# Turning 30 column groups of two up projections to tokens-as-rows, with VectorE squares and DMAs in front of the convolution

## The chip, the cores and the metric

One core of one Trainium2 chip runs the whole program in one launch. The metric is the device time of that launch in microseconds: the median of three runs of the kernel before is 1923.41 us (1923.33 to 1925.26). One further execution was taken by the hardware profiler. All durations in this document come from that profiled execution, and times in it are counted from the start of its span.

## What is computed

A trunk of two layers over 256 tokens and 2048 channels, all in float32. Each layer has a mixer (layer 0 pools over time, layer 1 attends), a residual and a layer norm, and then the part that the change is about: a gated feed-forward network with a causal convolution of width 3 over time between the up projection and the gate, again with a residual and a layer norm.

```python
def conv_ffn(h, w_up, conv_w, conv_b, w_down):
    S = h.shape[1]
    u = h @ w_up                                  # 256 x 2048 times 2048 x 11008
    up = jnp.pad(u, ((0, 0), (CONV_WIDTH - 1, 0), (0, 0)))
    c = conv_b + up[:, 0:S] * conv_w[0]
    for j in range(1, CONV_WIDTH):
        c = c + up[:, j:j + S] * conv_w[j]        # token t sees tokens t, t-1, t-2 of its own channel
    gate, val = jnp.split(c, 2, axis=-1)
    return (jax.nn.silu(gate) * val) @ w_down     # 256 x 5504 times 5504 x 2048
```

Products are as exact as float32: each weight and each activation is split into a high part and a low part, and three products (high by high, high by low, low by high) are added up in PSUM.

## The kernel before, in words

**Units and groups.** The work is a list of units. A unit is one piece of a weight matrix, mostly 512 rows by 512 columns (1 MB). Four units with the same 512 columns make a group, whose sums stay in PSUM until the last unit is done; then a function called `post` takes them out. Per unit, SyncE's queue loads the piece into one of three `raw` buffers (L69), ScalarE makes the high part `wh` (L86), VectorE the low part `wl` (L87), and TensorE multiplies. There are four `wh` and four `wl` buffers, so the split of unit i+3 is issued ahead of unit i, and it can start once TensorE has done unit i-1.

**Two forms of a group.** In the form with channels as rows (`group`, `mm_quad`, mode "ab"), the weight is what TensorE holds still: for each 128 x 128 block, L181 streams the high and the low half of the activations (512 columns), and L183 streams the high half past the low part of the weight (256 columns). The result has channels on partitions and tokens along the row, in four PSUM banks. In the form with tokens as rows (`group_tm`, `tm_block`), the activations are held still and the weight streams, three times 512 columns for each 128 channels and each half of the tokens (L206 to L208). The result has 128 tokens on partitions and 512 channels along the row, in two banks, t0 and t1. The up projections use the first form, the down projections (but for one) the second.

**The feed-forward part.** `ffn` runs up(0), up(1), up(2), then the down projection of their products, then up(3) to up(5) and their down projection, then 6 and 7, then 8 to 10. Each up(q) is two groups, the gate's and the value's. Here "gate q" and "value q" name them. `evac` brings the sums to an SBUF tile `u` (ScalarE copies the one half, L574, VectorE adds the other, L575), `conv` does the convolution (four L583 on ScalarE, eight L587 on VectorE), then SiLU on the gate (L599), gate times value (L620), and the split of the product into `g` (L266 on ScalarE, L262 on VectorE), which the down projection holds still.

**What sets the order.** Each engine does its instructions in the order in which the program lists them, and waits where it must. `later(n, f)` lists f behind the matmuls of the n-th unit from now; `before[i]` lists it ahead of those of unit i, behind the splits that `ahead(i)` lists. Value groups 2, 5, 7 and 10 come right ahead of a down projection, so their convolution is listed without delay (`later(0, ...)`, L626); the others follow one unit later. `turns` lets the first units of two down groups alternate: for up to three q's, the last q is first needed in the fourth unit, and for two q's (6 and 7) in the third.

**Layer norm.** `resid_last` ends in `chain` (L392 on): four small matmuls put mean and mean square into one PSUM bank, ScalarE squares and takes a root (L400, L402), and VectorE makes `rm` (L401, L403, L404). The next group's matmuls use that bank again, so they wait for L404, its last reader. The first groups behind a norm run in a mode "x" on values that are not yet normalised, and `norm_evac` (L439) puts mean and deviation in at the end.

**Existing turns.** `to_tokens` (L658) and `to_features` (L672) turn the residual between the two layouts: four VectorE transposes, each of 32 x 32 squares, into a tile, then 16 DMAs of 32 partitions each, issued by GpSimd, that put the squares in place.

Of the kernel before, what the change touches and what calls it, by code (L numbers as in the profile page):

```python
# [33 lines left out]
def trunk(ctx: ExitStack, tc: tile.TileContext, x, pool_w_in, pool_w_grp, pool_scale, pool_w_out,  # L34
# [102 lines left out]

    def phi(ps):
        return untwine(ps[:, :T])
# [124 lines left out]
    def split_act(dst, src):  # L264
        n = src.shape[1]
        A.copy(dst[:, 0:n, 0, :T], src)  # L266
        lo_part(dst, src, n)
# [7 lines left out]
    invd = const.tile([P, P], F32, name="invd")  # L275
    ones4 = const.tile([P, P], F32R, name="ones4")
# [72 lines left out]
    def shift(s, first, lay, which):  # L349
        ps = bank("shift")  # L350
        PE.matmul(ps[:, :T], ones4, s, start=True, stop=True)
        cs = lnp.tile([P, T], F32R, name="cs", tag="cs")
        A.copy(cs, ps[:, :T])
# [37 lines left out]
    def chain(ps, lay, which, after):  # L391
# [10 lines left out]
        A.activation(t2[:, 1, :], t2[:, 1, :], AF.Sqrt, bias=epst)  # L402
        V.reciprocal(rm[:, 0, :], t2[:, 1, :])  # L403
        V.tensor_tensor(rm[:, 1, :], mean, rm[:, 0, :], OP.mult)  # L404
        mb, rb = mr.to_broadcast([P, 4, T]), rs.to_broadcast([P, 4, T])
        g0 = 32 * which

        def spread():
            for i in range(4):
                PE.matmul(ps[:, i * P:i * P + P], one1, dg[:, i, :], start=True, stop=True)  # L410
            A.copy(rm.rearrange("p a t -> p (a t)"), ps)
            norm(0)
# [26 lines left out]
    def norm_evac(ps, nb, tmp, dst):  # L439
# [3 lines left out]
        for m0 in range(0, nb, 2):  # L443
            ts = [(m, tmp()) for m in range(m0, min(nb, m0 + 2))]
            for m, t in ts:
                V.tensor_tensor(apart2(t), phi(ps[m]), apart2(ST["rs"]), OP.mult)
            for m, t in ts:
                V.scalar_tensor_tensor(t, ST["mr"], wgb[:, m, 0:1], t, op0=OP.mult, op1=OP.subtract)
                A.activation(dst(m), t, AF.Identity, scale=-1.0, bias=wgb[:, m, 1:2])
# [15 lines left out]
    def pool_post(g):  # L465
        def post(ps):
# [3 lines left out]
            for m in range(4):  # L470
                pm = apart2(p[:, m, PADW:])
                A.copy(pm, phi(ps[m]))
                if g < 3:
                    V.tensor_tensor(pm, pm, plo(ps[m]), OP.add)
# [13 lines left out]
            def two():  # L488
                pooled_q[g] = quad_tile("pooled")
                split_act(pooled_q[g], po)  # L490
# [17 lines left out]
    def x_quad(q, halves=(0, 1)):  # L508
# [4 lines left out]
        for half in halves:  # L513
# [5 lines left out]
            pv2 = ps.rearrange("p (k t) -> p k t", k=2)  # L519
            s = slice(2 * half, 2 * half + 2)  # L520
            if q == 0 and half == 1:
                V.tensor_copy(XC[q][:, s, 0, :T], pv2)
            else:
                A.copy(XC[q][:, s, 0, :T], pv2)
            V.tensor_tensor(XC[q][:, s, 1, :T], pv2, XC[q][:, s, 0, :T].bitcast(F32), OP.subtract)
            before.setdefault(min(q + 1, 3), []).append(lambda s=s, pv2=pv2: A.copy(H[q][:, s, :], pv2))
# [26 lines left out]
    def ffn(lay):  # L553
# [3 lines left out]
        def pads():  # L557
            u = pools["ffn"].tile([P, 4, 2 + T], F32, name="u", tag="t4")
            V.memset(u[:, :, 0:2], 0.0)
            return u  # L560

        def evac(ps, nb, mode):
            fp = pools["ffn"]
            u = pads()

            def tmp():
                return fp.tile([P, T], F32, name="ut", tag="t1", bufs=4)

            if mode == "x":
                norm_evac(ps, nb, tmp, lambda m: u[:, m, 2:])  # L570
                return u
            for m in range(nb):
                t = apart2(tmp())
                A.copy(t, plo(ps[m]))  # L574
                V.tensor_tensor(apart2(u[:, m, 2:]), phi(ps[m]), t, OP.add)  # L575
            return u

        def conv(u, blk0, nb):
            cv = cvec[lay]
            c = pools["ffn"].tile([P, 4, T], F32, name="c", tag="t4")  # L580
            for m in range(nb):
                j = blk0 + m
                A.activation(c[:, m, :], u[:, m, 2:], AF.Identity, scale=cv[:, 2, j:j + 1], bias=cv[:, 3, j:j + 1])  # L583
            for i in (1, 0):
                for m in range(nb):
                    j = blk0 + m
                    V.scalar_tensor_tensor(c[:, m, :], u[:, m, i:i + T], cv[:, i, j:j + 1], c[:, m, :],  # L587
# [3 lines left out]
        def gate_post(q, nb, mode):  # L591
            def post(ps):
                u = evac(ps, nb, mode)

                def two():
                    c = conv(u, 4 * q, nb)

                    def three():
                        A.activation(c[:, :nb], c[:, :nb], AF.Silu)  # L599
                        gates[q] = c  # L600

                    later(1, three)

                later(1, two)
            return post

        def val_post(q, nb, mode):
            def post(ps):
                later(1 if q == 0 else 0, lambda: val_chain(q, nb, mode, ps))
            return post  # L610

        def val_chain(q, nb, mode, ps):
            u = evac(ps, nb, mode)

            def two():
                c = conv(u, NF + 4 * q, nb)

                def three():
                    s = gates.pop(q)
                    V.tensor_tensor(s[:, :nb], s[:, :nb], c[:, :nb], OP.mult)  # L620
                    gq[q] = quad_tile("g")
                    split_act(gq[q], s[:, :nb])
# [3 lines left out]
            later(0 if q in (2, 5, 7, 10) else 1, two)  # L626
# [65 lines left out]
    def store(c, t):  # L692
        nc.sync.dma_start(out[0, t * P:(t + 1) * P, 512 * c:512 * c + 512], HT[c][:, t, :])

    def tm_post(c, first, last, back=False):
        def post(t, ps, half=None):
# [6 lines left out]
            if back and t == 1:  # L703
                later(2 + 3 * c, lambda: to_features(c))
# [341 lines left out]
```

## Time and profile before

| | |
|---|---|
| median of 3 runs | 1923.41 us |
| the profiled execution's own time | 1923.13 us |
| its span, first to last instruction | 1921.3 us |
| granted TensorE clock | 1.000 |
| VectorE (DVE) busy | 1409.5 us, 73% |
| ScalarE (ACT) busy | 1012.8 us, 53% |
| GpSimd (POOL) busy | 176.1 us, 9% |
| DMA queue of SyncE | 381.71 MB, 59.3% of the 16 engines' time |

A row of the groups' table reads: line, engine, operation, output <- inputs, shape, count | busy us, mean ns of one | idle us of the engine ahead of them, and what ended the idle time. A row of a timeline reads: start us, us, engine, line, operation, count, and in brackets the idle time ahead and what ended it. In both, PE is TensorE, PEld its weight load, SPq the queue of SyncE. Matmuls overlap in their drawn durations, so their pace is read from start to start.

### The profile page before, as it was taken

To read this page: it belongs to the slowest core of one execution; us is meant where nothing else is said; L and a number is where in the kernel's file an instruction comes from. 1 tells how busy PE (TensorE), PEld (TensorE's weight loads), DVE (VectorE), ACT (ScalarE), POOL (GpSimd) and SP (SyncE) were. 2 spreads that over 40 slices of the span, in tenths; PEclk is the share of its full clock that TensorE was granted. 3 is DMA by queue.
4 is the path that set the end of the run, shared out by engine and by line. 5 is a ranking of instruction groups with operands and counts; after the bars stand their busy time and mean duration, and the time that the engine had idled before them with its cause. 6 is when DMAs were issued, how large, how long until landed. Compare 5 with 4: busy or idle time off the path is not lost.

```text
span 1921.3 us, 28253 instructions
## 1 busy us (share of the span) xinstructions
PE 1914.9 (100%) x11542; PEld 1748.8 (91%) x11542; DVE 1409.5 (73%) x1760; ACT 1012.8 (53%) x1115; POOL 176.1 (9%) x326
## 2 busy tenths in 40 slices
PE   9999999999999999999999999999999999999999
PEld 9999999899989989999989889999889988989997
DVE  7869888757755767789876767888756765775677
ACT  6545675445535535555644445576535543544553
POOL 2000003300000033000033210001410000000000
PEclk9999999999999999999999999999999999999999
DMA  8665557765565576656566655556865566555564
GB/s 279 227 205 197 176 192 246 231 208 198 197 217 200 188 231 212 197 181 219 174 216 214 201 167 193 189 189 206 252 221 197 198 204 212 198 197 200 184 213 148
DMA packets 204513, 392.61 MB, mean 204 GB/s; under 512 B 11630, under 2 KB 22020, under 8 KB 204128
## 3 DMA queue, kind: packets, MB, share of 16 engines
q1 hardware_dynamic: 194240, 381.71, 59.3%
q0 software_dynamic: 10144, 9.11, 2.3%
q8 instruction: 90, 1.47, 0.3%
q14 instruction: 39, 0.32, 0.0%
HBM read 380.01 MB, written 2.10 MB: 199 GB/s over the span
## 4 chain that ended last, share of the span: by engine, by line
PE 97%; DVE 2%; DMA 0%; issue 0%; SPq 0%; ACT 0%; DVEq 0%
PE acc L181 42%; PE acc L183 21%; PE t L206 8%; PE t L207 8%; PE t L208 8%; PE acc L187 2%; PE acc L185 2%; PE acc L186 2%; DVE wl L87 1%; PE acc L172 0%; PE o L894 0%; PE s L835 0%; DVE xp L386 0%; DMA raw<-in_pool_w_in_dram 0%; DVE fold L325 0%
## 5 line engine op out<-in xcount | busy, mean ns | idle before, releaser
L87 DVE TENSOR_TENSOR wl<-raw,wh 128x2048 fp32r<-128x2048 f32 (+2 forms) x374 | 815.6, 2187 | 398.2 <-ACT wh L86 397.4
L181 PE MATMUL acc<-xc,wh 128*128 128x512 f32 x3072 | 1009.1, 383 | 0.0
L86 ACT CAST wh<-raw 128x2048 fp32r<-128x2048 f32 (+2 forms) x374 | 679.7, 1825 | 484.3 <-PE acc L181 214.0
L183 PE MATMUL acc<-xc,wl 128*128 128x256 f32 x3072 | 835.6, 272 | 0.0
L181 PEld LDWEIGHTS acc<-xc,wh 128*128 128x128 f32 x3072 | 577.6, 188 | 83.6 <-DVE o L897 0.5
L183 PEld LDWEIGHTS acc<-xc,wl 128*128 128x128 f32 x3072 | 589.8, 192 | 0.4
L206 PE MATMUL t<-wh,g 128*128 128x512 f32 x590 | 222.8, 378 | 0.0
L207 PE MATMUL t<-wl,g 128*128 128x512 f32 x590 | 222.8, 378 | 0.0
L208 PE MATMUL t<-wh,g 128*128 128x512 f32 x590 | 222.8, 378 | 0.0
L587 DVE SCALAR_TENSOR_TENSOR c<-u,cv,c 128x256 f32<-128x256 f32 x344 | 141.9, 479 | 0.6
L208 PEld LDWEIGHTS t<-wh,g 128*128 128x128 f32 x590 | 111.5, 189 | 15.6
L206 PEld LDWEIGHTS t<-wh,g 128*128 128x128 f32 x590 | 111.5, 189 | 15.6
L207 PEld LDWEIGHTS t<-wl,g 128*128 128x128 f32 x590 | 111.6, 189 | 15.5
L669 POOL DMA_DIRECT2D ht<-hb x128 | 73.7, 583 | 563.5 <-DVE hb L663 497.5
L185 PE MATMUL acc<-xp,wh 128*128 128x258 f32 x384 | 105.7, 275 | 0.8 <-DVE rm L404 0.8
L186 PE MATMUL acc<-xp,wh 128*128 128x258 f32 x384 | 105.7, 275 | 0.0
L187 PE MATMUL acc<-xp,wl 128*128 128x258 f32 x384 | 105.2, 274 | 0.0
L574 ACT COPY ut<-acc 128x256 f32<-128x256 f32 x156 | 56.2, 372 | 81.5 <-PE acc L183 81.5
L583 ACT ACTIVATE c<-u,cv 128x256 f32<-128x256 f32 x172 | 89.4, 594 | 0.4 <-DVE u L575 0.4
L181 PE MATMUL acc<-o,wh 128*128 128x512 f32 x256 | 84.5, 383 | 0.0
L181 PE MATMUL acc<-mixed,wh 128*128 128x512 f32 x256 | 84.0, 382 | 0.0
L185 PEld LDWEIGHTS acc<-xp,wh 128*128 128x128 f32 x384 | 72.9, 190 | 1.0 <-DVE rm L404 1.0
(220 smaller groups left out, 1985.8 us busy)
## 6 DMA issues: line engine op xcount, KB each, us to landing
raw<-in_ffn_w_up_dram SPq DMA_DIRECT2D x160, 1024.0 KB, 4.9
raw<-in_ffn_w_down_dram SPq DMA_DIRECT2D x80, 1024.0 KB, 5.2
raw<-in_pool_w_out_dram SPq DMA_DIRECT2D x16, 1024.0 KB, 5.1
raw<-in_shared_w_k_dram SPq DMA_DIRECT2D x16, 1024.0 KB, 5.1
raw<-in_attn_w_q_dram SPq DMA_DIRECT2D x16, 1024.0 KB, 5.4
raw<-in_shared_w_v_dram SPq DMA_DIRECT2D x16, 1024.0 KB, 5.7
raw<-in_attn_w_o_dram SPq DMA_DIRECT2D x16, 1024.0 KB, 5.2
raw<-in_pool_w_in_dram SPq DMA_DIRECT2D x12, 1024.0 KB, 6.6
```

The costliest lines, as they stand in the source:

```text
L86: A.copy(h, r)
L87: V.tensor_tensor(l, r, h.bitcast(F32), OP.subtract)
L181: PE.matmul(ps[m], h[:, k, c], q[:, k, :, :T].rearrange("p l (a c) -> p l c a", a=2), start=st, stop=False)
L183: PE.matmul(ps[m][:, :T], l[:, k, c], cols(k, 0), start=False, stop=sp)
L185: PE.matmul(ps[m][:, :n], h[:, k, c], cols(k, 0), start=st, stop=False)
L186: PE.matmul(ps[m][:, :n], h[:, k, c], cols(k, 1), start=False, stop=False)
L187: PE.matmul(ps[m][:, :n], l[:, k, c], cols(k, 0), start=False, stop=sp)
L206: PE.matmul(ps, xh, hk, start=first and k == 0, stop=False)
L207: PE.matmul(ps, xh, lk, start=False, stop=False)
L208: PE.matmul(ps, xl, hk, start=False, stop=last and k == nk - 1)
L583: A.activation(c[:, m, :], u[:, m, 2:], AF.Identity, scale=cv[:, 2, j:j + 1], bias=cv[:, 3, j:j + 1])
L587: V.scalar_tensor_tensor(c[:, m, :], u[:, m, i:i + T], cv[:, i, j:j + 1], c[:, m, :], op0=OP.mult, op1=OP.add)
```

## The change

In both layers, 15 of the 22 groups of the up projection take the form with tokens as rows: the gates of q = 1 to 9 and the values of q = 1, 3, 4, 6, 8 and 9. Groups of q = 0 (mode "x") and of q = 10 (narrower), and the values 2, 5 and 7, stay as they were.

A group with tokens as rows has to be turned for the convolution. `turn_up` transposes 32 x 32 squares out of the two PSUM banks into a tile `b` (four VectorE transposes), then issues 16 DMAs on GpSimd's queue, 32 KB each, into `u`. The convolution of such a group is listed four units later, so behind the whole of the next group.

So that the DMAs move long runs, tokens are held in another order everywhere: within each 128, token 4k+j stands at place 32j+k. A tile `u` has six runs of 64 columns: a token's predecessor stands one run ahead, and two extra runs at the start are filled by one new ScalarE copy per group. Loading, pooling, masks and the final store follow that order; pooling goes through plain token order and back. The split of products is done in two halves of the tokens.

Besides, the root of the norm at the end of layer 0 (`which == 1`) is listed ahead of the next unit's matmuls instead of at once; `ut` takes two buffers instead of four; ones4 goes; `to_features` is listed at units 2, 5, 7, 10 instead of 2, 5, 8, 11; and pool sizes change.

```diff
@@ chain @@
-        A.activation(t2[:, 1, :], t2[:, 1, :], AF.Sqrt, bias=epst)
-        V.reciprocal(rm[:, 0, :], t2[:, 1, :])
-        V.tensor_tensor(rm[:, 1, :], mean, rm[:, 0, :], OP.mult)
+        def root():
+            A.activation(t2[:, 1, :], t2[:, 1, :], AF.Sqrt, bias=epst)
+            V.reciprocal(rm[:, 0, :], t2[:, 1, :])
+            V.tensor_tensor(rm[:, 1, :], mean, rm[:, 0, :], OP.mult)
+
+        if which == 0:
+            root()
+        else:
+            before.setdefault(state["done"] + 1, []).append(root)
@@ split of a product @@
-    def split_act(dst, src):
+    def split_half(dst, t, src):
         n = src.shape[1]
-        A.copy(dst[:, 0:n, 0, :T], src)
-        lo_part(dst, src, n)
+        h, l = (dst[:, 0:n, i, t * P:t * P + P].rearrange("p m (j k) -> p m j k", j=4) for i in range(2))
+        A.copy(h, src)
+        V.tensor_tensor(l, src, h.bitcast(F32), OP.subtract)
@@ ffn @@
+        def turn_up(u):
+            b = pools["ffn"].tile([P, 4, 4, 2, 32], F32, name="b", tag="b", bufs=1)
+
+            def part(t, ps):
+                src = ps.rearrange("p (h i b a) -> p a h i b", a=2, h=2, i=4)
+                dst = b[:, :, :, t, :].rearrange("p i (a h) b -> p a h i b", a=2)
+                for a in range(2):
+                    V.transpose(dst[:, a], src[:, a])
+
+            def move():
+                v = b.rearrange("p i m t b -> p i (m t b)")
+                w = u.rearrange("p j m q -> p j (m q)")
+                for i in range(4):
+                    for j in range(4):
+                        nc.gpsimd.dma_start(w[32 * i:32 * i + 32, 2 + j, :], v[32 * j:32 * j + 32, i, :])
+            return part, move
 
         def conv(u, blk0, nb):
             cv = cvec[lay]
-            c = pools["ffn"].tile([P, 4, T], F32, name="c", tag="t4")
+            A.copy(u[:, 0:2, 0:nb, 1:], u[:, 4:6, 0:nb, :63])
+            c = pools["ffn"].tile([P, 4, 4, 64], F32, name="c", tag="c")
...
+        def post_tokens(q, chain):
+            st = []
+
+            def post(t, ps):
+                if t == 0:
+                    u = runs()
+                    st.extend([u, *turn_up(u)])
+                st[1](t, ps)
+                if t == 1:
+                    st[2]()
+                    chain(q, 4, st[0], 4)
+            return post
 
         def up(q):
             nb = min(4, NF - 4 * q)
-            x0 = q == 0
-            mode = "x" if x0 else "ab"
-            group(w_up, rows4, 512 * q, nb * P, psrcs if x0 else xsrcs, gate_post(q, nb, mode),
-                  mode=mode)
-            group(w_up, rows4, FF + 512 * q, nb * P, psrcs if x0 else xsrcs, val_post(q, nb, mode),
-                  mode=mode)
+            mode = "x" if q == 0 else "ab"
+            for c0, chain in ((512 * q, gate_chain), (FF + 512 * q, val_chain)):
+                if q > 0 and nb == 4 and (chain == gate_chain or q not in (2, 5, 7)):
+                    group_tm(w_up, rows4, c0, 512, xsrcs, post_tokens(q, chain))
+                    continue
+                n = 1 if chain == gate_chain or q not in (2, 5, 7, 10) else 0
+                post = post_features(q, nb, mode, chain, n)
```

**How instructions move, place 1: VectorE around the end of value 7 in layer 0**, right ahead of the down projection of 6 and 7. Before, from the split of the last unit that is listed ahead, to the low half of `g`:

```order
L87 TENSOR_TENSOR wl_6115<-raw_6035,wh_6114 128x2048
L559 MEMSET u 128x4x2
L575 TENSOR_TENSOR u<-acc,ut 128x256 x4
L587 SCALAR_TENSOR_TENSOR c<-u,cv_592,c 128x256 x8
L87 TENSOR_TENSOR wl_6180<-raw_6074,wh_6179 128x2048
L620 TENSOR_TENSOR c<-c 128x1024
L262 TENSOR_TENSOR g<-c,g 128x4x256
```

The same stretch in the changed kernel (L621 is the convolution, L591 the evacuation, L643 gate times value, L274 the low half):

```order
L87 TENSOR_TENSOR wl_5860<-raw_5781,wh_5859 128x2048
L621 SCALAR_TENSOR_TENSOR c<-u,cv_590,c 128x4x64 x8
L568 MEMSET u 128x8
L591 TENSOR_TENSOR u<-acc,ut 128x2x4x32 x4
L621 SCALAR_TENSOR_TENSOR c<-u,cv_590,c 128x4x64 x8
L87 TENSOR_TENSOR wl_5940<-raw_5819,wh_5939 128x2048
L643 TENSOR_TENSOR c<-c 128x1024
L274 TENSOR_TENSOR g<-c,g 128x4x128 x2
```

The first eight convolution steps there are those of gate 7, which came 15 us earlier before; they now stand between the split and the evacuation of value 7. Values 2 and 5 have the same order. On ScalarE the same place holds, in the changed kernel:

```order
L86 CAST wh_5859<-raw_5781 128x2048
L613 COPY u<-u 128x8x63
L617 ACTIVATE c<-u,cv_590 128x4x64 x4
L590 COPY ut<-acc 128x256 x4
L613 COPY u<-u 128x8x63
L617 ACTIVATE c<-u,cv_590 128x4x64 x4
L86 CAST wh_5939<-raw_5819 128x2048
L630 ACTIVATE c<-c 128x1024
L273 CAST g<-c 128x4x128 x2
```

The new copy L613 stands ahead of each set of four L617, and the gate's SiLU (L630) has moved behind the next split.

**Place 2: the norm at the end of layer 0.** Before, ScalarE has, around the square and the root of the variance:

```order
L86 CAST wh_8246<-raw_8107 128x2048
L86 CAST wh_8300<-raw_8180 128x2048
L400 ACTIVATE var<-acc 128x256
L402 ACTIVATE var<-var,epst 128x256
L86 CAST wh_8365<-raw_8244 128x2048
L86 CAST wh_8422<-raw_8298 128x2048
```

In the changed kernel:

```order
L86 CAST wh_7921<-raw_7782 128x2048
L86 CAST wh_7975<-raw_7855 128x2048
L405 ACTIVATE var<-acc 128x256
L86 CAST wh_8037<-raw_7919 128x2048
L409 ACTIVATE var<-var,epst 128x256
L86 CAST wh_8097<-raw_7973 128x2048
```

One split has moved between the square and the root. VectorE has the same there, with the low half of that split between the variance and the reciprocal:

```order
L87 TENSOR_TENSOR wl_7976<-raw_7855,wh_7975 128x2048
L406 TENSOR_TENSOR var<-acc,var 128x256
L87 TENSOR_TENSOR wl_8038<-raw_7919,wh_8037 128x2048
L410 RECIPROCAL rm<-var 128x256
L411 TENSOR_TENSOR rm<-acc,rm 128x256
```

Before, L401, L403 and L404 followed each other directly, and that split came behind them.

**Place 3: GpSimd's queue, from the first feed-forward part to the second.** The changed kernel has, besides loads of constants:

```order
L608 DMA u<-b 32x256 x32
L713 DMA ht<-hb 32x8x32 x16
L608 DMA u<-b 32x256 x16
L713 DMA ht<-hb 32x8x32 x32
L1040 IOTA mk 32x128 x4
L713 DMA ht<-hb 32x8x32 x16
L1040 IOTA mk 32x128 x8
L608 DMA u<-b 32x256 x128
L726 DMA h<-fb 32x8x32 x32
```

Before, the rows of `u` (L608) were not there and the 64 moves of `ht` followed each other with three IOTAs among them. The moves of gate 2 (the second L608 row) now stand behind the first 16 moves of `ht`.

More of the change, by code (lines that the diff above doesn't have):

```diff
@@ L350, in shift @@
         ps = bank("shift")
-        PE.matmul(ps[:, :T], ones4, s, start=True, stop=True)
+        PE.matmul(ps[:, :T], invr, s, start=True, stop=True)
         cs = lnp.tile([P, T], F32R, name="cs", tag="cs")
-        A.copy(cs, ps[:, :T])
+        A.activation(cs, ps[:, :T], AF.Copy, scale=4.0)
         cb = cs.bitcast(F32).unsqueeze(1).to_broadcast([P, 4, T])
@@ L489, in two @@
                 pooled_q[g] = quad_tile("pooled")
-                split_act(pooled_q[g], po)
+                for t in range(2):
+                    split_half(pooled_q[g], t, po[:, :, t * P:t * P + P].rearrange("p m (k j) -> p m j k", j=4))
             later(1, two)
@@ L586, in conv, with gate_chain, two, three @@
                     j = blk0 + m
-                    V.scalar_tensor_tensor(c[:, m, :], u[:, m, i:i + T], cv[:, i, j:j + 1], c[:, m, :],
+                    V.scalar_tensor_tensor(c[:, :, m], u[:, i:i + 4, m], cv[:, i, j:j + 1], c[:, :, m],
                                            op0=OP.mult, op1=OP.add)
             return c
[L591 to L613, printed above, removed]
+        def gate_chain(q, nb, u, n):
+            def two():
+                c = conv(u, 4 * q, nb)
+                def three():
+                    A.activation(c[:, :, :nb], c[:, :, :nb], AF.Silu)
+                    gates[q] = c
+                later(1, three)
+            later(n, two)
+        def val_chain(q, nb, u, n):
             def two():
@@ L619, in three, with post_features @@
                     s = gates.pop(q)
-                    V.tensor_tensor(s[:, :nb], s[:, :nb], c[:, :nb], OP.mult)
+                    V.tensor_tensor(s[:, :, :nb], s[:, :, :nb], c[:, :, :nb], OP.mult)
                     gq[q] = quad_tile("g")
-                    split_act(gq[q], s[:, :nb])
+                    for t in range(2):
+                        split_half(gq[q], t, s[:, :, :nb, 32 * t:32 * t + 32].rearrange("p j m k -> p m j k"))
                 later(1, three)
-            later(0 if q in (2, 5, 7, 10) else 1, two)
+            later(n, two)
+        def post_features(q, nb, mode, chain, n):
+            return lambda ps: chain(q, nb, evac(ps, nb, mode), n)
+        def post_tokens(q, chain):
+            st = []
+            def post(t, ps):
+                if t == 0:
+                    u = runs()
+                    st.extend([u, *turn_up(u)])
[4 more added lines that the diff above has]
+            return post
         def up(q):
             nb = min(4, NF - 4 * q)
-            x0 = q == 0
-            mode = "x" if x0 else "ab"
-            group(w_up, rows4, 512 * q, nb * P, psrcs if x0 else xsrcs, gate_post(q, nb, mode),
-                  mode=mode)
-            group(w_up, rows4, FF + 512 * q, nb * P, psrcs if x0 else xsrcs, val_post(q, nb, mode),
-                  mode=mode)
+            mode = "x" if q == 0 else "ab"
[5 more added lines that the diff above has]
+                post = post_features(q, nb, mode, chain, n)
+                if q == 0 and chain == val_chain:
+                    post = lambda ps, post=post: later(1, lambda: post(ps))
+                group(w_up, rows4, c0, nb * P, psrcs if q == 0 else xsrcs, post, mode=mode)
         def down(qs, last=False):
@@ L692, in store @@
     def store(c, t):
-        nc.sync.dma_start(out[0, t * P:(t + 1) * P, 512 * c:512 * c + 512], HT[c][:, t, :])
+        rows = out[0, t * P:(t + 1) * P, 512 * c:512 * c + 512].rearrange("(k j) c -> j k c", j=4)
+        nc.sync.dma_start(rows, HT[c][:, t, :])
     def tm_post(c, first, last, back=False):
@@ L912, in trunk @@
     with tc.tile_pool(name="start", bufs=1) as stp:
+        invd = stp.tile([P, P], F32, name="invd")
         for q in range(NQ):
@@ L979, in late_consts @@
             cvec.append(t)
-        A.copy(invr, invd)
         A.copy(identr, ident)
```

78 lines of the change are left out of this document (40 added, 38 removed).

## The prediction

> **What bounds the kernel now.** I read the page's busy times first, then the chain of work that ended last.
>
> ```profile
> PE 1914.9 (100%) x11542; PEld 1748.8 (91%) x11542; DVE 1409.5 (73%) x1760; ACT 1012.8 (53%) x1115; POOL 176.1 (9%) x326
> ...
> PE 97%; DVE 2%; DMA 0%; issue 0%; SPq 0%; ACT 0%; DVEq 0%
> ```
>
> TensorE is busy throughout and carries 97% of the chain. So time moves in two ways only: the matmuls themselves take longer or shorter, or TensorE is made to wait. For the first, two stretches of the chain give the pace from start to start, one in an up projection in the form with channels as rows, one in a down projection with tokens as rows.
>
> ```profile
> 845.45 0.22 PE acc L181
> ...
> 857.24 0.22 PE acc L181
> 330.87 0.21 PE t L208
> ...
> 342.96 0.22 PE t L207
> ```
>
> The first pair of rows stands 36 steps of one L181 with its L183 apart: 11.79 us / 36 = 0.3275 us. The second stands 56 matmuls apart: 12.09 / 56 = 0.2159 us. A group of 2048 x 512 weights is 64 such steps in the one form, 64 x 0.3275 = 20.96 us, and 16 x 2 x 3 = 96 matmuls in the other, 96 x 0.2159 = 20.73 us. All other terms are waits, so the question is which of the new lists keeps TensorE waiting.
>
> **The change part by part.**
>
> **Pitch.** 15 groups in each of two layers go from 20.96 to 20.72 us: 30 x 0.24 = **7.2 us gained**. The Trainium skill, page "TensorE: Matmul & The Clock Gate", section "Back-to-back issue gap", speaks against this: by its isolated gap of N/2.4 + 2.5 ns a pair of 512 and 256 columns would take 325.0 ns and three times 512 columns 215.8 each, an estimated gain of 64 x 0.325 - 96 x 0.2158 = 0.08 us a group, 2.5 in all. The trace has 327.5 ns in the pair and 215.9 in the other form, so the rule holds for the one and not for the other, and I go by the rows.
>
> **The root at the end of layer 0.** The rows are those of ScalarE, VectorE and TensorE in turn.
>
> ```profile
> 898.11 0.52 ACT L402 ACTIVATE var<-var,epst 128x256 f32<-128x256 f32 x1 [3.71 <-DVE var L401]
> 898.53 1.89 ACT L86 CAST wh<-raw 128x2048 fp32r<-128x2048 f32 x1
> ```
>
> ```profile
> 898.66 1.75 DVE L403 RECIPROCAL rm<-var 128x256 f32<-128x256 f32 x1 [0.58 <-ACT var L402]
> 900.45 0.42 DVE L404 TENSOR_TENSOR rm<-acc,rm 128x256 f32<-128x256 f32 x1
> 900.79 2.28 DVE L87 TENSOR_TENSOR wl<-raw,wh 128x2048 fp32r<-128x2048 f32 x1
> ```
>
> ```profile
> 900.93 0.38 PE L185 MATMUL acc<-xp,wh 128*128 128x258 f32 x1 [0.78 <-DVE rm L404]
> ```
>
> TensorE already waits 0.78 us for L404 and goes on at 900.93. In the changed list one split stands ahead of the root on ScalarE (1.89) and ahead of the reciprocal on VectorE (2.28). The load of that split is shown by the view of the tile raw in this stretch:
>
> ```profile
> L69 SPq DMA_DIRECT2D raw<-in_attn_w_q_dram x2: 368/368/368, 892.7 to 895.6; - x2
> DMA to landing us min/median/max: 5.1/5.2/6.9
> ```
>
> Issued at 892.7, it lands at 897.8. Then the cast is done at 899.75, the root at 900.2, the low half at 902.0, the reciprocal at 903.8 and L404 at 904.2; TensorE goes on 0.05 later, at 904.25: **3.3 us lost**. If the data were there earlier, only VectorE's 2.28 less the 0.58 that it idles now would be added, 1.7; with the slowest landing of that view some 4. Behind the root on ScalarE stand only further splits, three units ahead of need.
>
> **Value 7, both layers.** The rows are those of layer 0: VectorE, then ScalarE, then TensorE.
>
> ```profile
> 659.08 2.29 DVE L87 TENSOR_TENSOR wl<-raw,wh 128x2048 fp32r<-128x2048 f32 x1 [2.95 <-ACT wh L86]
> ...
> 663.41 3.54 DVE L587 SCALAR_TENSOR_TENSOR c<-u,cv,c 128x256 f32<-128x256 f32 x8
> 666.87 2.29 DVE L87 TENSOR_TENSOR wl<-raw,wh 128x2048 fp32r<-128x2048 f32 x1
> 669.07 1.22 DVE L620 TENSOR_TENSOR c<-c 128x1024 f32<-128x1024 f32 x1
> 671.41 1.23 DVE L262 TENSOR_TENSOR g<-c,g 128x1024 fp32r<-128x1024 f32 x1 [1.12 <-ACT g L266]
> ```
>
> ```profile
> 670.32 1.05 ACT L266 CAST g<-c 128x1024 fp32r<-128x1024 f32 x1 [3.69 <-DVE c L620]
> ```
>
> ```profile
> 672.61 0.38 PE L206 MATMUL t<-wh,g 128*128 128x512 f32 x1
> ...
> 673.04 0.38 PE L208 MATMUL t<-wh,g 128*128 128x512 f32 x1
> ```
>
> The product of q = 7 is ready at 671.4 (high) and 672.64 (low); the third unit of the down projection wants them at 672.61 and 673.04, 0.4 us of margin at the low half. In the changed list the eight steps of gate 7's convolution (3.54 us) stand between the split and the evacuation of value 7, and ScalarE has its new copy ahead of the convolution. The sizes:
>
> ```profile
> L526 ACT COPY h<-xT 128x512 f32<-128x512 f32 x8 | 4.2, 586 | 0.0
> L525 DVE TENSOR_TENSOR xc<-xT,xc 128x512 fp32r<-128x512 f32 x8 | 5.3, 688 | 9.4 <-ACT xc L524 9.4
> ```
>
> The copy has 504 columns, so near 0.58 us, like L526; half of a product has 512, so 0.59 for its high part and 0.69 for its low one. The convolution of value 7 then starts at 663.41 + 3.54 + 0.58 = 667.5, the split behind it ends at 673.2, the product at 674.4, the first high half at 675.0, its low half at 675.75. TensorE starts 2.4 us late and the third matmul, wanted at 675.5, another 0.3: 2.8 us. For two layers **5.6 lost**. If some of gate 7's steps run in what VectorE idles now (2.95 us ahead of the split at 659.08, which it cannot use for steps listed behind that split) the loss falls to 1.8 each; with the two buffers of `ut` and the copy both in the path it is 4.5.
>
> **The first value group behind an x group (value 1, third unit).** There VectorE is full.
>
> ```profile
> 257.66 0.74 DVE L446 TENSOR_TENSOR ut<-acc,rm 128x256 f32<-128x256 f32 x2
> ...
> 273.33 2.29 DVE L87 TENSOR_TENSOR wl<-raw,wh 128x2048 fp32r<-128x2048 f32 x1 [0.58 <-ACT wh L86]
> ```
>
> ```profile
> 276.15 0.27 PE L183 MATMUL acc<-xc,wl 128*128 128x256 f32 x1
> ```
>
> The split ends at 275.62, wanted at 276.15. With two `ut` buffers L446 waits for ScalarE to empty one, and the copy stands ahead of each convolution: about 0.35 + 0.35 + 0.58 = 1.3 later, less the 0.53 of margin: 0.7, in two layers **1.4 lost** (0 to 1.5 each).
>
> **The turns of q = 2 and 5.** Each turned group adds 16 DMAs of 32 KB on GpSimd. The nearest rows are the moves of the residual, on GpSimd's queue and, last, by the table of DMA issues (KB each, us to landing).
>
> ```profile
> 318.84 0.58 POOL L669 DMA_DIRECT2D ht<-hb  x1 [8.87 <-issue]
> ...
> 329.09 1.16 POOL L669 DMA_DIRECT2D ht<-hb  x2 [0.90 <-DMA ht<-hb]
> ```
>
> ```profile
> ht<-hb POOLq DMA_DIRECT2D x128, 32.0 KB, 4.8
> ```
>
> 16 of them take 11.4 us to issue and 4.8 to land, some 16 from the group's end. The convolution is listed four units (20.7 us) later, so ScalarE, whose copy waits for all 16 with the splits of three units later queued behind it, finds them there; and VectorE's next transposes, which need `b` again, come a group later. At q = 5 this holds. At q = 2 the queue starts late (the feed-forward part's first groups are the full stretch above), and gate 2's moves stand behind 16 of `ht`: moves of gate 1 about 279 to 291, value 1 to 310, then 11 of `ht` (as above), then gate 2 at 317 to 330, against 326.4 when ScalarE wants it. The 3.5 us that ScalarE then stands pass to the product less the 2 us by which it is early: 1.5 each, **3.0 lost** in two layers, 0 to 4 each.
>
> **At nothing.** 4 transposes replace 4 adds on VectorE:
>
> ```profile
> L575 DVE TENSOR_TENSOR u<-acc,ut 128x256 f32<-128x256 f32 x156 | 58.1, 416 | 17.6 <-ACT ut L574 17.6
> L663 DVE STREAM_TRANSPOSE hb<-h 128x256 f32<-128x256 f32 x32 | 11.3, 411 | 3.7 <-DMA ht<-hb 3.7
> ```
>
> 4 x 0.411 for 4 x 0.416. ScalarE loses four copies and gets one, with 47% of its time free; the 15.7 MB of moves join 392 MB on queues 59% in use, under loads issued three units (15 us) ahead. Without that cover each late set would hold ScalarE and cost like q = 2. At the start and in pooling, reads and writes step 16 bytes. No row of before has such a step; L575 reads PSUM in 8-byte steps at the pace of contiguous rows, so I take nothing, and a doubling as the other end: two x quads with two L525 and two L526-sized copies each, 2 x 2 x (0.586 + 0.688) = 5.1 us.
>
> **Sum:** -7.2 + 3.3 + 5.6 + 1.4 + 3.0 = **+6.1**, from 1923.13 (the profiled execution's own time, 0.28 under the median) to **1929.2**. All low ends give 1921, all high ends 1940.
>
> **The rivals.**
>
> **No waits at the down projections.** If gate 7's steps find VectorE idle, and the moves are in time, only pitch and root remain: -3.9, 1919.2. It is decided by whether the first high half of product 7 is written before TensorE wants it, 1.2 us later than it is now. For it speaks that VectorE idles 27% of the time, against it that the listed order leaves that idling in front of the split. Chance 0.2; this is the case on the other side.
>
> **Moves land late.** If the 16 moves take 3 us longer than `ht`'s (11.4 + 4.8), each set holds ScalarE and the splits behind it; at q = 2 and 5 in two layers some 2 to 3 us more, four times: 1937 to 1940. Against it: 20.7 us of room. Chance 0.12.
>
> **Steps of 16 bytes are slow.** If they double as above, 1934.3. [...] Chance 0.05.
>
> **No gain of pitch.** If weights stream more slowly past held activations in an up group than in a down group, at the 0.3275 x 64 / 96 = 0.2183 us that makes both forms equal, the 7.2 is gone: 1936.4. Against it: both kinds of group read their operands from the same kinds of buffers. Chance 0.03. By the isolated gap of the Trainium skill's page named above, 2.5 would be left of the 7.2, an estimate that gives 1933.9.
>
> **How the numbers follow.** The sum as worked out has 0.6. The range takes the rival without waits at its lower edge and half of that of late moves: 1919 to 1936. What a measurement can tell is about 0.2%, 3.85 us: faster is under 1919.56, slower over 1927.26. Of the main case some 0.14 lies within and 0.46 above; of the rival without waits 0.15 below and 0.05 within; the others lie above, but for 0.02 kept for a gain beyond these: faster 0.17, same 0.19, slower 0.64.
>
> **What would show it.** In the profile after: a pace of 0.216 us in the 30 groups; TensorE waiting 3 to 4 us for L411 instead of 0.78; waits of 2 to 3 us for `g` at the third unit of the down projection of 6 and 7 in both layers; a wait for a low half at value 1's third unit; ScalarE idle ahead of its new copy for the DMAs at q = 2 and nowhere else. I am wrong if TensorE's waits add to under 6 us, or if it waits for splits in steady state.

## The result and the profile after

| | before | changed |
|---|---|---|
| median | 1923.43 us (6 runs) | 1984.62 us (6 runs, 1979.90 to 1987.23) |
| ratio of the runs | | 1.0314, 95% interval 1.0299 to 1.0328 |
| span of the profiled execution | 1921.3 us | 1982.7 us |
| mean granted clock of TensorE | 1.000 | 0.987 |

The changed kernel is 61 us slower, ten times what was forecast (+6.1) and far above the range. The page after, in the lines that were shown of before:

```profile
PE 1926.9 (97%) x10582; PEld 1728.1 (87%) x10582; DVE 1423.6 (72%) x1786; ACT 1009.7 (51%) x1064; POOL 412.9 (21%) x815
...
PE 64%; DVE 8%; DMA 6%; issue 3%; ACT 2%; POOL 2%; ACTq 0%; DVEq 0%; POOLq 0%
```

VectorE has 14 us more work than before, ScalarE 3 us less. But the chain that ended last, which was 97% TensorE, now runs through VectorE, DMAs, ScalarE and GpSimd too. The list of TensorE's waits (us in total, times, longest):

```profile
PE t L212 <- ACT g L273: 22.6, 4, 8.7
PE acc L189 <- DVE wl L87: 5.0, 4, 1.8
PE t L213 <- DVE wl L87: 4.2, 4, 1.8
PE acc L191 <- DVE rm L411: 4.2, 1, 4.2
PE acc L187 <- ACT wh L86: 2.8, 2, 2.0
```

With the smaller ones this is 42.0 us; before had 2.2. Four waits for the product `g` (q = 2 and 7 in both layers) are the largest part. The others are for splits (`wh`, `wl`), which came late, and for the late root. Next to the waits stands a second loss. Here are stretches around and behind three of them, by the view of windows (stretch, length, busy times; the granted clock is the number behind POOL's count), the first pair around the root, the second behind the waits for `g` at 683 and 1412:

```profile
925.00:931.00 6.00, 1.79 (x15) 1.60 (x14) 4.88 (x4) 3.37 (x3) 0.00 (x0) 0.83 0.89 304
931.00:936.00 5.00, 5.00 (x26) 5.00 (x26) 4.96 (x4) 3.04 (x5) 0.00 (x0) 0.53 0.39 147
...
688.50:694.00 5.50, 5.16 (x14) 4.12 (x15) 4.15 (x4) 4.41 (x4) 0.00 (x0) 0.55 0.49 184
...
1421.50:1428.00 6.50, 6.05 (x16) 4.84 (x17) 5.05 (x4) 6.32 (x5) 0.00 (x0) 0.56 0.49 166
```

TensorE is busy again, but at a clock of 0.53 to 0.56 for some 5 us: 5.0 x 0.47 = 2.4, 5.5 x 0.45 = 2.5 and 6.5 x 0.44 = 2.9 us more. Seven such stretches, read in the same way, add up to some 14 us, an estimate. The Trainium skill, page "TensorE: Matmul & The Clock Gate", section "Part 1: The HAM clock gate", has it that an idle window of some 3.4 us puts the array at half clock; the trace agrees, with 0.53 behind a wait of 4.2 us. Shorter waits are less regular. In the run nomove below TensorE waits 2.12 us at the same place of both layers: behind the first the clock is 0.55 for 3.3 us (674.7 to 678.0), behind the second 1.00 (1716.7 to 1720.0). The 3.4 us are thus no safe lower limit here.

The third loss is at the end: the last matmuls that stand in the chain of before, then those of the changed kernel.

```profile
1913.95 1.99 PE w L763 x4
```

```profile
1965.64 1.99 PE w L808 x4
```

From their ends to the ends of the spans are 1921.3 - 1915.9 = 5.4 us and 1982.7 - 1967.6 = 15.1 us: 9.7 more. It is the last store that takes them. SyncE's issues of the eight stores, before and changed:

```profile
1903.55 14.85 SPq L693 DMA_DIRECT2D out_dram<-ht  x8
```

```profile
1955.23 15.58 SPq L738 DMA_DIRECT2D out_dram<-ht  x8
```

From the end of the last issue to the end of the span are 2.9 us before (1921.3 - 1918.4) and 11.9 us in the changed kernel (1982.7 - 1970.8).

The pitch did fall, as two rows of a turned group 69 matmuls apart show: 14.89 / 69 = 0.2158 us.

```profile
1559.78 0.38 PE L214 MATMUL t<-wh,xc 128*128 128x512 f32 x1
...
1574.67 0.38 PE L214 MATMUL t<-wh,xc 128*128 128x512 f32 x1
```

So: waits +39.8, half clock +14, tail +9.7, pitch -7.2, together 56 of 61.4 us. Where the other 5 went stays open.

**How the waits for g come about** shows best at q = 1 and 2 of layer 0. GpSimd, ScalarE and VectorE:

```profile
303.30 5.37 POOL L608 DMA_DIRECT2D u<-b  x11 [11.88 <-issue]
310.68 0.50 POOL L608 DMA_DIRECT2D u<-b  x1 [2.00 <-DMA u<-b]
311.73 1.96 POOL L608 DMA_DIRECT2D u<-b  x4 [0.56 <-DMA u<-b]
```

```profile
318.75 0.61 ACT L613 COPY u<-u 128x504 f32<-128x504 f32 x1 [5.09 <-DMA u<-b]
```

```profile
300.98 0.43 DVE L601 STREAM_TRANSPOSE b<-t 128x256 f32<-128x256 f32 x1
...
319.90 3.54 DVE L621 SCALAR_TENSOR_TENSOR c<-u,cv,c 128x256 f32<-128x256 f32 x8 [3.92 <-ACT c L617]
323.38 0.44 DVE L601 STREAM_TRANSPOSE b<-t 128x256 f32<-128x256 f32 x1
```

Value 1 is transposed at 300.98. GpSimd issues 11 moves, then one, then four, each time behind earlier ones that must land. The last lands just ahead of 318.75, where ScalarE has stood for 5.1 us with the next splits behind it in its list. The convolution follows, and only behind it, in VectorE's list, the transposes of gate 2. From transpose to transpose are 323.38 - 300.98 = 22.4 us, while a group lasts 20.7. **It is a loop** (transposes, moves, copy, convolution, next transposes) that is longer than the pitch by 1.7 us. So lateness grows here from group to group. Gate 2's moves, behind those of `ht` on GpSimd, come later still; then the product of q = 2 is due, and TensorE waits 7 us.

### The profile page after: what moved, and what is told of

Same layout as the page of the kernel before. It is cut to its first block, busy times and chain, and to the rows that moved or that the text cites. A ratio compares the mean times of both kernels' runs of the same rounds, so it can differ in the third digit from the quotient of the medians.

```text
span 1982.7 us, 27019 instructions
## 1 busy us (share of the span) xinstructions
PE 1926.9 (97%) x10582; PEld 1728.1 (87%) x10582; DVE 1423.6 (72%) x1786; ACT 1009.7 (51%) x1064; POOL 412.9 (21%) x815
## 4 chain that ended last, share of the span: by engine, by line
PE 64%; DVE 8%; DMA 6%; issue 3%; ACT 2%; POOL 2%; ACTq 0%; DVEq 0%; POOLq 0%
PE t L212 16%; PE t L214 16%; PE t L213 16%; PE acc L187 10%; PE acc L189 5%; DMA u<-b 5%; DVE c L621 2%; DVE wl L87 2%; POOL u L608 2%; ACT wh L86 1%; DMA ht<-hb 1%; ACT c L617 0%; DVE c L643 0%; PE acc L191 0%; DVE xp L391 0%
## 5 line engine op out<-in xcount | busy, mean ns | idle before, releaser
L608 POOL DMA_DIRECT2D u<-b x480 | 235.1, 498 | 1054.9 <-DVE b L601 761.9
L213 PE MATMUL t<-wl,xc 128*128 128x512 f32 x1088 | 412.7, 379 | 1.9 <-DVE u L568 1.2
L212 PE MATMUL t<-wh,xc 128*128 128x512 f32 x1088 | 413.3, 380 | 0.0
L214 PE MATMUL t<-wh,xc 128*128 128x512 f32 x1088 | 412.4, 379 | 0.0
L187 PE MATMUL acc<-xc,wh 128*128 128x512 f32 x1152 | 380.5, 383 | 0.8 <-ACT wh L86 0.8
L189 PE MATMUL acc<-xc,wl 128*128 128x256 f32 x1152 | 313.7, 272 | 3.1 <-DVE wl L87 3.1
L212 PE MATMUL t<-wh,g 128*128 128x512 f32 x590 | 227.4, 385 | 23.4 <-ACT g L273 22.6
L187 PEld LDWEIGHTS acc<-xc,wh 128*128 128x128 f32 x1152 | 216.7, 188 | 32.3 <-ACT wh L86 1.0
L213 PEld LDWEIGHTS t<-wl,xc 128*128 128x128 f32 x1088 | 205.7, 189 | 31.9 <-DVE u L568 2.0
L214 PEld LDWEIGHTS t<-wh,xc 128*128 128x128 f32 x1088 | 205.7, 189 | 29.0
L212 PEld LDWEIGHTS t<-wh,xc 128*128 128x128 f32 x1088 | 205.7, 189 | 29.0
L214 PE MATMUL t<-wh,g 128*128 128x512 f32 x590 | 226.8, 384 | 0.0
L189 PEld LDWEIGHTS acc<-xc,wl 128*128 128x128 f32 x1152 | 221.2, 192 | 4.4 <-DVE wl L87 4.0
L621 DVE SCALAR_TENSOR_TENSOR c<-u,cv,c 128x256 f32<-128x256 f32 x344 | 145.8, 479 | 50.0 <-ACT c L617 49.1
L213 PEld LDWEIGHTS t<-wl,g 128*128 128x128 f32 x590 | 114.0, 193 | 20.7 <-DVE wl L87 4.5
```

Of the source, the lines that this page charges most:

```text
L187: PE.matmul(ps[m], h[:, k, c], q[:, k, :, :T].rearrange("p l (a c) -> p l c a", a=2), start=st, stop=False)
L189: PE.matmul(ps[m][:, :T], l[:, k, c], cols(k, 0), start=False, stop=sp)
L212: PE.matmul(ps, xh, hk, start=first and k == 0, stop=False)
L213: PE.matmul(ps, xh, lk, start=False, stop=False)
L214: PE.matmul(ps, xl, hk, start=False, stop=last and k == nk - 1)
L608: nc.gpsimd.dma_start(w[32 * i:32 * i + 32, 2 + j, :], v[32 * j:32 * j + 32, i, :])
```

## The experiments

Theory A says that the loss is the DMAs of the turns, which the order of the lists closes to a loop. Rival B says that it is the order and the work on VectorE and ScalarE alone. Each run stands with its median, its ratio to the kernel before and the 95% interval of the ratio.

**nomove** leaves the 16 DMAs out; the data of the turned groups land in wrong places.

```diff
-                dst = b[:, :, :, t, :].rearrange("p i (a h) b -> p a h i b", a=2)
+                dst = u[:, 2:6, :, 32 * t:32 * t + 32].rearrange("p i (a h) b -> p a h i b", a=2)
...
-                        nc.gpsimd.dma_start(w[32 * i:32 * i + 32, 2 + j, :], v[32 * j:32 * j + 32, i, :])
```

> The 16 DMAs per turned group are left out; VectorE writes the turned squares straight into u, in wrong places, so the convolution reads the same shapes of data without waiting for a DMA. Theory A (the loss is the time the DMAs take to land, which holds ScalarE's copy, VectorE's next transposes and so the product that the down projection wants): the waits for g at q = 2 (7.0 and 8.9 us) and at the third down projection (6.8 in layer 0, 3.0 in layer 1) go with their spells of half clock; the late root (4.4 + 2.6) stays and q = 7 keeps some 2 us of wait a layer: 1930 to 1938 us. Rival B (the order of the lists and the added work on VectorE and ScalarE, not the DMAs): the waits at q = 2 stay over 4 us and the time stays over 1955 us.

1940.67 us, 1.0089 [1.0074, 1.0104]: 44 us of the 61 go with the moves, and rival B falls. The time is 2.7 us above the range that A expected; A had named no tail, and nomove keeps it (15.1 us). Waits for `g` are left at q = 7 only, in VectorE's and ScalarE's lists:

```profile
667.13 3.54 DVE L615 SCALAR_TENSOR_TENSOR c<-u,cv,c 128x256 f32<-128x256 f32 x8 [1.18 <-ACT c L611]
```

```profile
674.04 1.14 ACT L273 CAST g<-c 128x512 fp32r<-128x512 f32 x2 [2.72 <-DVE c L637]
```

```profile
PE t L212 <- ACT g L273: 4.2, 2, 2.1
PE t L213 <- DVE wl L87: 1.2, 2, 0.6
```

The last line is value 1's wait for a low half, 0.6 us a layer. The rows ahead of it are the prediction's step for value 7 almost to the tenth: convolution at 667.13 (forecast 667.5), wait 2.1 us (forecast 2.4 for the high half).

**half and twelve** keep the bytes and change the count of DMAs to 8 and 12 (8 x 64 KB; 8 x 32 and 4 x 64 KB), with blocks in wrong places. The lines below are those of half; twelve does the same for two of the four values of i.

```diff
-                    for j in range(4):
-                        nc.gpsimd.dma_start(w[32 * i:32 * i + 32, 2 + j, :], v[32 * j:32 * j + 32, i, :])
+                    for j in range(2):
+                        nc.gpsimd.dma_start(w[32 * i:32 * i + 32, 2 + 2 * j:4 + 2 * j, :], v[32 * i:32 * i + 32, 2 * j:2 * j + 2, :])
```

> The changed kernel with 8 DMAs of 64 KB per turned group instead of 16 of 32 KB: the same bytes, laid down in wrong places, so that the output is not the reference's. If the count sets how late a turned group lands (0.5 us of issue each, and a stop behind the twelfth until earlier ones have landed), a set shrinks from 15.3 us to 8 or 10, the loop to some 16 us a group, and the time falls to 1945 to 1962 us. If bytes, or the 1 MB loads that share the engines, set it, it stays over 1972.

> The changed kernel with 12 DMAs per turned group instead of 16: eight of 32 KB and four of 64 KB, the same bytes, four of them laid down in wrong places. With 16 GpSimd issues 11 or 12, stops until the first have landed, and issues the rest; with 8 (the run half) the time fell to 1942. If the stop behind the twelfth is what counts, 12 come close to 8: 1942 to 1952 us. If each DMA's 0.5 us of issue counts, the time lies half way, 1960 to 1968. If neither, it stays over 1975.

half: 1942.35 us, 1.0097 [1.0082, 1.0112], as fast as with no moves. twelve: 1954.39, 1.0158 [1.0143, 1.0173], between its two cases and nearer to the stop. ScalarE's waits for the moves in the changed kernel, in twelve and in half:

```profile
ACT u L613 <- DMA u<-b: 58.3, 17, 8.1
```

```profile
ACT u L617 <- DMA u<-b: 20.8, 9, 6.3
```

```profile
ACT u L613 <- DMA u<-b: 0.7, 1, 0.7
```

The sum of the bytes is not what makes the moves late. Fewer DMAs are faster: the issue of 8 takes 3.9 us, that of 16 took 10.4 with the stops (303.30 to 313.69). The larger DMAs also move rows of 2 KB instead of 1 KB and keep them on their partitions; these runs don't tell that apart from the count.

**swap** lists the transposes ahead of the convolution of the group before (`first` is set for groups that are turned).

```diff
+            if post is not None and getattr(post, "first", False):
+                post()
+                post = None
             for p in ready:
                 p[1]()
```

> The transposes of a turned group are listed ahead of the convolution of the group before it instead of behind it; nothing else changes. Theory L (a loop: moves of group n, then its convolution, then the transposes of group n+1, 22.4 us a turn in the trace against a pitch of 20.7): the loop loses the convolution, the turns shrink to some 17 us, and the waits at q = 2 fall from 7.0 and 8.9 us to under 3 each, those at the third down projection too: 1950 to 1968 us. Rival Q (GpSimd's queue: the moves of ht stand ahead of gate 2's): the moves of gate 2 still end near 340 us of layer 0 and the time stays over 1975 us.

1957.78 us, 1.0184 [1.0167, 1.0201]: 27 us come back by order alone, within the range that the loop gave. ScalarE's waits for the moves fall to 28.9 us, TensorE's for `g` to 13.7, and those for splits are nearly gone. At q = 2 the waits for `g` stayed at 3.8 and 5.4 us, over the 3 that was expected.

**noht** asks why. It is fix (below) with the residual's moves left out.

```diff
-        b = lnp.tile([P, 4, T], F32, name="hb", tag="sq")
-        b = b.rearrange("p a t -> p (a t)").rearrange("p (j t m b) -> p j t m b", j=4, t=2, m=4)
+        b = v.rearrange("p t c -> p (t c)").rearrange("p (j t m b) -> p j t m b", j=4, t=2, m=4)
...
-                nc.gpsimd.dma_start(dst[32 * j:32 * j + 32, :, i, :], src[32 * i:32 * i + 32, j])
```

> fix (transposes first, root at once, stores as four DMAs), and the 64 moves of the residual ht per layer left out: VectorE writes its squares straight into ht, in wrong places, so the output is not the reference's. Theory Q (at q = 2 the moves of ht stand ahead of gate 2's on GpSimd): the waits of 4.0 and 6.2 us at q = 2 that fix keeps, and the 4 us of half clock behind them, shrink to under 2.5 us each as at q = 7: 1934 to 1940 us from 1948.3. Rival N (the list alone: gate 2's convolution between the split and value 2's evacuation): both waits stay over 3.5 us and the time over 1944.

1933.65 us, 1.0052 [1.0038, 1.0065], 14.7 under fix and just under the range's lower edge. In fix GpSimd had, ahead of gate 2's moves:

```profile
308.18 4.60 POOL L719 DMA_DIRECT2D ht<-hb  x8 [2.25 <-DMA u<-b]
...
318.26 1.02 POOL L613 DMA_DIRECT2D u<-b  x2
320.87 6.98 POOL L613 DMA_DIRECT2D u<-b  x14 [1.59 <-DMA ht<-hb]
```

In noht they begin at 315.97, and the wait at q = 2 falls from 3.4 to 1.1 us in layer 0 and from 6.1 us to under 0.4 in layer 1. The queue that place 3 showed is the second cause at q = 2.

**gates** gives gates 2, 5 and 7 their old form.

```diff
-                if q > 0 and nb == 4 and (chain == gate_chain or q not in (2, 5, 7)):
+                if q > 0 and nb == 4 and q not in (2, 5, 7):
```

> Gates 2, 5 and 7 go back to the form with channels as rows, so no turned group stands right ahead of values 2, 5 and 7; all else as changed. Theory A (turned gate right ahead of a value whose product is wanted at once): the waits at q = 2 and q = 7 (about 32 us with their half clock) go, 6 x 0.24 = 1.4 us of pitch is given back, the waits at the third down projection and at the root stay: 1950 to 1960 us. Rival C (turned groups are late wherever they stand after the first x group): the wait only moves to value 1 and the time stays over 1970 us.

1974.42 us, 1.0265 [1.0249, 1.0280]: the time is the one of rival C. The waits for `g` fell from 22.6 to 3.9 us, and those for splits rose:

```profile
PE acc L189 <- DVE wl L87: 8.3, 6, 1.8
PE t L213 <- DVE wl L87: 5.7, 3, 2.0
PE t L212 <- ACT wh L86: 4.6, 3, 2.0
```

They did not go to value 1, as C had it: the largest part stands at value 2 and the first units of the down projection behind it (327 to 337 us in layer 0), most of the rest around the start of the last down projection. While the loop runs, lateness comes out somewhere; taking the place away where it showed didn't cure it.

**before_root** puts the late root alone into the kernel before; **store** changes the final stores of the changed kernel.

```diff
-        nc.sync.dma_start(rows, HT[c][:, t, :])
+        for j in range(4):
+            nc.sync.dma_start(rows[j], HT[c][32 * j:32 * j + 32, t, :])
```

> The kernel before with one edit: the root of the norm at the end of layer 0 is listed ahead of the next unit's matmuls, as in the change. As the prediction had it, TensorE waits 3.3 us longer and nothing more: 1926.7 us. With a spell of half clock behind the wait, as the trace of the change shows (0.53 granted for 5 us), another 2.4 to 2.6: 1929 to 1930 us.

> The changed kernel with one edit: each final store of 128 tokens x 512 channels goes out as four DMAs of 32 partitions instead of one DMA with the tokens reordered inside it. The profile after has 12.6 us between the issue of the last store and the end, 3.2 before (its page shows no landing time for these stores). Theory: the reordered store is spread over few of the 16 DMA engines; four plain ones are spread over all, cost three more issues of some 0.35 us each behind the last product, and take 7 to 9 us off: 1975 to 1978 us. Rival: the scattered rows themselves are slow to write; the time stays within 2 us of the changed kernel's 1984.6.

before_root: 1928.62 us, 1.0026 [1.0017, 1.0035], 5.2 us lost. TensorE waits 4.3 us instead of 0.8, and the next stretch runs at 0.71:

```profile
904.48 0.58 PE L185 MATMUL acc<-xp,wh 128*128 128x258 f32 x1 [4.29 <-DVE rm L405]
```

```profile
905.00:909.00 4.00, 4.00 (x28) 4.00 (x27) 3.97 (x4) 2.12 (x5) 0.00 (x0) 0.71 0.45 175
```

So 3.5 us of wait and some 1.2 of clock; the wait was forecast, the clock not. store: 1978.48 us, half a us above its range and 6 less than the changed kernel, on the edge of what its spread (1975.8 to 1982.4) can tell. Its trace is plainer: from the same matmuls to the end 1980.6 - 1970.75 = 9.9 us, against 15.1.

**fix** is swap, the root at once, and store together. **fix_gates** is fix with gates.

> Three edits together: transposes listed ahead of the convolution of the group before (swap), the root of layer 0's norm at once, the final stores as four DMAs each. If the three causes are separate, they add up: 1957.8 - 5.5 - 8 = 1944 us, 1941 to 1947. If removing one wait only exposes the next, over 1950.

> The same three edits, and gates 2, 5 and 7 back in the form with channels as rows. The waits for g at q = 2 and q = 7 that swap leaves (4.0 and 5.9, 2.3 and 3.0 us, with 8.2 us of half clock behind them) should go, against 1.4 us of pitch: 1920 to 1926 us. If turned groups that stand further ahead of a product hold ScalarE as well (as gates alone showed, where waits for splits took the place of those for g), 1930 or more.

fix: 1948.32, 1.0127 [1.0112, 1.0143], 1.3 over its range's upper end. fix_gates: 1930.99, 1.0038 [1.0024, 1.0053], 5 over its range's upper end, at the 1930 where the second reading began: waits of 0.8 us for `g` had stayed (behind them the clock is 1.00, so no half clock goes with them), and the tail was still 9.8 us.

**spq** moves half of the DMAs to SyncE's queue. **best_a** and **best_b** have it beside fix and fix_gates, with the stores on two queues.

```diff
-                        nc.gpsimd.dma_start(w[32 * i:32 * i + 32, 2 + j, :], v[32 * j:32 * j + 32, i, :])
+                        q = nc.gpsimd if j < 2 else nc.sync
+                        q.dma_start(w[32 * i:32 * i + 32, 2 + j, :], v[32 * j:32 * j + 32, i, :])
...
-            nc.sync.dma_start(rows[j], HT[c][32 * j:32 * j + 32, t, :])
+            (nc.sync if j % 2 else nc.scalar).dma_start(rows[j], HT[c][32 * j:32 * j + 32, t, :])
```

> The changed kernel with 8 of each group's 16 moves issued by SyncE, on the queue of the loads, and 8 by GpSimd; the right data in the right places. If GpSimd's queue is what makes the turns late, this does what half did: 1942 to 1955 us. If the moves hold up the loads behind them on SyncE (they wait for the transposes), new waits for splits appear and the time stays over 1960.

> swap, root at once, stores as four DMAs each on two queues (SyncE and ScalarE), and the moves half on SyncE; all 30 groups still turned. From fix, 1948.3: the waits at q = 2 go (4.0 + 6.2 us and 3.9 of half clock), the tail gets some 4 us shorter, q = 7 keeps its waits of 2.7 and 3.1 us with 3.3 of half clock: 1928 to 1933 us. If SyncE's moves delay the loads, over 1940.

> As best_a, with gates 2, 5 and 7 in the form with channels as rows. From fix_gates, 1931.0: some 4 us off the tail and up to 2 us off the short waits at the down projections: 1924 to 1928 us, so still not faster than the kernel before (1923.4), because the pitch left to gain is 24 x 0.24 = 5.8 us and the waits at value 1 (0.8 each), for g (0.9 each) and the longer tail take more than that. Under 1921 if the rest of the waits goes as well.

All three came out slow. spq (2011.66, 1.0459 [1.0442, 1.0477]) and best_a (1945.11, 1.0113 [1.0098, 1.0128]) lie where their expectations put the case that the moves hold up the loads. best_b (1938.57, 1.0075 [1.0060, 1.0091]) is 11 us over its range and 7.6 slower than fix_gates. ScalarE's wait for loads, in the changed kernel and in spq:

```profile
ACT wh L86 <- DMA raw<-in_ffn_w_up_dram: 45.9, 12, 7.8
```

```profile
ACT wh L86 <- DMA raw<-in_ffn_w_up_dram: 218.6, 49, 10.8
```

On SyncE's queue the moves wait for the transposes (216 us in all in spq), and the loads stand behind them in the same list.

**best_d** is fix_gates with the two queues for the stores, and with the products of values 2, 5 and 7 listed earlier and that of value 0 later; **best_e** is the same with all 30 groups turned and SiLU of gates 2, 5 and 7 listed at once. The line below is from the value's chain.

```diff
-                later(1, three)
+                later(0 if q in (2, 5, 7) else 2 if q == 0 else 1, three)
```

> fix_gates with three more edits: stores' four DMAs on two queues, the product of values 2, 5 and 7 listed ahead of the next split instead of behind it, that of value 0 one unit later. From fix_gates, 1931.0: tail 3.1 us shorter, three waits for g of 0.8 us with 0.4 of half clock each gone (3.7), the waits of 0.9 us in value 1 gone in both layers (1.8): 1922.4, between 1920.5 and 1924.5. If the gain of pitch (24 x 0.24 = 5.8 us) is real and all other losses are named, it cannot stay over 1926; if it isn't, 1927 or more.

> As best_d, but with all 30 groups turned (gates 2, 5 and 7 too), and SiLU of these gates listed at once. From fix, 1948.3: tail 3.1 and value 1 1.8 us less; the waits for g at q = 2 and 7 (4.0, 6.2, 2.7, 3.1 us) shorter by the split's 2.3 us each and their half clock by some 4 us in all: 1930 to 1935 us. If it comes under best_d, the turned gates are no loss any more.

best_d: 1924.02 us (11 runs, 1921.31 to 1926.28), 1.0004 [0.9995, 1.0012]: as fast as the kernel before, as expected. Its waits, of which none is for `g` or in value 1 any more:

```profile
PE acc L181 <- ACT wh L86: 1.4, 1, 1.4
PE warm L985 <- DVE epst L987: 1.1, 1, 1.1
PE acc L194 <- DVE rm L416: 0.8, 1, 0.8
```

The profiled execution is the fastest of the 11. In it the account closes: span 1921.3, less 24 x 0.24 = 5.8 of pitch, plus 2.5 of waits (4.7 against 2.2) and 1.5 of tail (6.9 against 5.4), is 1919.5, which is the measured span. So the gain of pitch is real. The median is 2.7 us higher, and best_d as a whole is no faster than the kernel before. best_e: 1939.15, 1.0078 [1.0063, 1.0094], 4 over its range: against fix, waits for `g` fell from 14.2 to 3.0 us, and those for splits, most of them at q = 2, rose to 7.7 and 4.9.

## Why the prediction was wrong

**The bound and the pitch** were right. TensorE was the bound; the turned groups run at 0.216 us per matmul, and the account of best_d closes with the 0.24 us a group. The isolated gap of the Trainium skill (page "TensorE: Matmul & The Clock Gate", section "Back-to-back issue gap"), by which an estimated 2.5 of the 7.2 us would be left, was rightly passed over.

**The step that failed is "The turns of q = 2 and 5"**, put at 3.0 us. One set was sized nearly right: "some 16 from the group's end" against 318.75 - 300.98 = 17.8 here. But it was laid against a room of 20.7 us as if each set began at its own group's end. That VectorE's list has the convolution of one group in front of the transposes of the next stands in neither the sum nor the rivals. By the rows, transposes, moves, copy and convolution follow each other around: 22.4 us against 20.7. With 16.2 us for a set (11.4 + 4.8) and the 4.6 from its copy to the next transposes (323.38 - 318.75) the way around would be 20.8, just at the pitch; so the path that was overlooked left no room, and the 1.6 us by which a set was longer made it late. "VectorE's next transposes ... come a group later" said that they would not be held; swap shows that they were (27 us). The length of a set, with GpSimd's stops in it (half), and `ht` in front of gate 2 (noht) are the other causes, which overlap with the order. The sum of this step has a slip as well: a set that begins at 317 ends, with its 11.4 and 4.8 us, at 333 and not at 330. One of the prediction's signs of being wrong, waits for splits, is in the trace with 12 us (5.0 + 4.2 + 2.8). The rival "Moves land late" named this cause and had 0.12, but priced it at 8 to 11 us, for four places and without what follows. Late in the last up projections of layer 0, for example, ScalarE stood before the copy of value 9,

```profile
826.64 0.61 ACT L613 COPY u<-u 128x504 f32<-128x504 f32 x1 [8.09 <-DMA u<-b]
```

and the splits behind it came late: between 832 and 844 us TensorE waits four times for splits, 5.9 us in all, a wait that no step had.

**No step had the half clock** behind a wait, some 14 us; each pause of TensorE was priced as its length alone.

**The final store** is in no term of the sum, "At nothing" included: it cost 9.7 us. store gets 5 of them back in the trace, best_d 8. The Trainium skill, page "DMA: Bandwidth & Descriptors", section "Rules for kernel authors", says that an outermost dimension of fewer than 16 confines a DMA to that many engines; the reordered store has 4 outermost. That agrees with the tail, though no view here shows a store's engines.

**The root** was sized well: 3.3 us forecast, 3.5 of wait in before_root. **Value 7** too: 2.8 a layer forecast, 2.1 of wait in nomove. **Value 1** as well: 0.7 a layer forecast, 0.6 in nomove. **Transposes and the new copy**: 416 ns for 411, 612 ns for some 580.

## What to carry to other kernels

Where an engine works through a fixed list, a new step that waits for a DMA must be followed around: from its result through every list back to its own next start. If that loop is longer than the pitch of the work, lateness adds up, whatever each step costs alone. A wait of TensorE can cost more than its length, as each one of 4.2 us and more in the changed kernel did, and taking away the place where lateness shows can move it to the next one.

## What had not been expected of the hardware

In this kernel steps of 16 bytes cost about double where they lie in SBUF and nothing where they lie in PSUM. The groups by form, of the changed kernel: the split of a product half in contiguous runs, the same size with 16-byte steps in pooling, and the low part at the start, which reads PSUM in 16-byte steps.

```profile
L273 ACT CAST g<-c 128x512 fp32r<-128x512 f32 x40 | 22.8, 618 | 81.9 <-DVE c L643 81.9
...
L273 ACT CAST pooled<-po 128x512 fp32r<-128x512 f32 x8 | 11.0, 1432 | 14.8 <-DVE po L491 14.8
...
L533 DVE TENSOR_TENSOR xc<-xT,xc 128x512 fp32r<-128x512 f32 x8 | 5.3, 688 | 9.1 <-ACT xc L532 9.1
```

It is 1432 ns against 618 on ScalarE; and the low part takes 688 ns, the same as before the change. The rival on 16-byte steps was right on SBUF, but had put its price where PSUM is read; TensorE's only sign of it is under 1 us in the first 50.
